# Attention stage of a two-layer encoder: the rotation in six operations over all ten heads, and the low halves of later input units subtracted on POOL

## The chip, the cores and the metric

The kernel runs on one core of one Trainium2 chip. A core has four compute engines, each with an instruction queue of its own that is worked off in order: PE (TensorE, the matrix unit), DVE (VectorE), ACT (ScalarE) and POOL (GpSimd). DMA transfers are issued from a queue too, here from SP (SyncE) and from POOL. The metric is device time of one execution in microseconds, the median over runs of the kernel.

## The reference, cut to what matters

The network has two layers. Layer 0 projects a modulated input `h = x * (1 + scale) + shift` once and feeds windowed attention, a spatial gate and a gating path from it; layer 1 is a bidirectional recurrence. The change touches layer 0: how `h` is split into two parts, and the rotation of queries and keys.

```python
S, D_MODEL, HEAD_DIM, N_Q_HEADS, N_KV_HEADS = 2048, 1024, 64, 8, 2
ROPE_DIM = HEAD_DIM // 4            # 16: only the first 16 of a head's 64 columns turn

def partial_rotary(t, positions):
    half = ROPE_DIM // 2
    ang = positions.astype(jnp.float32)[:, :, None, None] * inv_freq
    cos, sin = jnp.cos(ang), jnp.sin(ang)
    t1, t2 = tr[..., :half], tr[..., half:]
    rot = jnp.concatenate([t1 * cos - t2 * sin, t2 * cos + t1 * sin], axis=-1)
    return jnp.concatenate([rot.astype(t.dtype), t[..., ROPE_DIM:]], axis=-1)

def even_mixer(h, positions, w_in, w_out, sink, ...):
    q, k, v, su, sv, g = jnp.split(h @ w_in, EVEN_SPLITS, axis=-1)
    q = partial_rotary(q.reshape(B, S, N_Q_HEADS, HEAD_DIM), positions)
    k = partial_rotary(k.reshape(B, S, N_KV_HEADS, HEAD_DIM), positions)
    y_attn = windowed_gqa_sink(q, k, v, sink)      # |i - j| <= 128, softmax with a sink per head
    y_sg = chunked_spatial_gating(su, sv, ...)
    y = jnp.concatenate([y_attn, y_sg], axis=-1) * jax.nn.silu(g)
    return y @ w_out
```

## The kernel before, in words

All products of 32-bit numbers are made from two parts: a number is split into a high part `hi` (rounded to the matrix unit's fp32r type) and a low part `lo`, the number less `hi`. The helper `split` (L147) writes `hi` on ACT and `lo` on DVE, and `mm3` (L151) adds three matmuls, hi by hi (L152), hi by lo (L153) and lo by hi (L154).

Attention works on 16 blocks of 128 tokens. Its parts are:

- `build(u)` makes the input unit `u`, which is 256 tokens or two blocks: in four pieces of 256 features it loads x (L319), transposes it on PE (L325), applies scale and shift on ACT into the tile `hm` (two buffers), splits it into `hhi` and `hlo`, and stores both to memory for a later stage (L336, queue SP). There are eight units.
- `project(blk)` multiplies a block's `hi` and `lo` by the weights: keys and values first (`pk`, 256 columns), then the eight query heads (`pq`, 512 columns). ACT copies the results into the tile `qk`, heads 0 to 7 queries and 8 to 9 keys. DVE rotates 16 columns of each head (L365 to L370), in six operations for the two key heads and then six for the eight query heads. The keys are split into `ks` (L374 on ACT, L375 on DVE), transposed on PE (L379) and copied to `kT` (L387).
- `scores(blk)` splits and transposes the queries (L411 to L415), multiplies them by the keys (L422, L423), and makes the softmax: DVE takes mask and minimum (L424), ACT the exponential (L427), DVE the division (L434). DVE then transposes in squares of 32 (L452), and 16 DMAs move the squares from T to P (L459), for blocks 0 to 10 half of them issued by SP and half by POOL, for later blocks all by SP. Blocks 14 and 15 are transposed on PE instead (L444).
- `values(blk)` multiplies by the values (L469), copies out on ACT (L477), and POOL issues the store (L479).

The order in the text, from L494 on, is: units 0 and 1 are built during the setup together with the modulation and the split of the weights; then for each block in turn `scores(blk + 1)`, for even blocks `build((blk + 4) // 2)`, `values(blk)`, `project(blk + 3)`. This is not the order of each engine's queue: `schedule_with_timeline_sim=True` (L1194) lets a planner, which follows a model of the times, place the instructions of every queue before the program is made. What a queue holds is then fixed.

Once attention's projections are over, the loads of `h` for the next stage start (L521, L522), behind what stands in SP's queue. The later stages are the spatial gate with the output projection, and the recurrence of layer 1.

Of the kernel before, what the change touches and what calls it, by code (L numbers as in the profile page):

```python
# [7 lines left out]
F32 = mybir.dt.float32  # L8
F32R = mybir.dt.float32r
I32 = mybir.dt.int32  # L10
AF = mybir.ActivationFunctionType
ALU = mybir.AluOpType
# [41 lines left out]
def kernel(  # L54
# [27 lines left out]
    nc = tc.nc  # L82
    act = nc.scalar.activation
    tt = nc.vector.tensor_tensor
# [9 lines left out]
    def pool(stack, name, side=None, bufs=1, space=None):  # L94
        kw = {} if space is None else {"space": space}
        if side is not None:
            kw["side"] = side
        return stack.enter_context(tc.tile_pool(name=name, bufs=bufs, reuse_waits="tile", **kw))
# [48 lines left out]
    def split(hi, lo, src):  # L147
        act(out=hi, in_=src, func=AF.Copy)  # L148
        tt(out=lo, in0=src, in1=hi.bitcast(F32), op=ALU.subtract)  # L149

    def mm3(ps, ahi, alo, bhi, blo, first, last):  # L151
        nc.tensor.matmul(ps, lhsT=ahi, rhs=bhi, start=first, stop=False)  # L152
        nc.tensor.matmul(ps, lhsT=ahi, rhs=blo, start=False, stop=False)  # L153
        nc.tensor.matmul(ps, lhsT=alo, rhs=bhi, start=False, stop=last)  # L154

    def bank(p, tag, shape=(128, C)):
        t = p.tile(list(shape), F32, tag=tag, name=tag)
        return t
# [74 lines left out]
    for i in range(2):  # L233
        nc.gpsimd.dma_start(out=vrow0[24 + 8 * i:32 + 8 * i].rearrange("k (a q) -> k a q", a=4),
                            in_=ada_b[1, i * D:i * D + D].rearrange("(a k q) -> k a q", a=4, q=32))
# [22 lines left out]
    cos_t = ap.tile([128, 16, 8], F32, name="cos_t")  # L258
    sin_t = ap.tile([128, 16, 8], F32, name="sin_t")
# [43 lines left out]
    def k_place(n, p):  # L303
        if n not in kTs:
            kTs[n] = ap.tile([128, 4, 768], F32R, tag="kT", bufs=2, name="kT")
        return kTs[n][:, :, p * 128:p * 128 + 128]
# [7 lines left out]
    def build(u, part=range(4)):  # L314
        t, uu = divmod(u, 2)
        hT = hTs.setdefault(u, ([], []))
        for k2 in part:
            xp = jp.tile([128, 2, 256], F32, tag="xp", bufs=2, name="xp")
            load(out=xp, in_=xs[u * 256:u * 256 + 256, k2 * 256:k2 * 256 + 256].rearrange("(b p) f -> p b f", p=128))  # L319
            hi = jp.tile([128, 2, 256], F32R, tag="act", bufs=18, name="hhi")  # L320
            lo = jp.tile([128, 2, 256], F32R, tag="act", bufs=18, name="hlo")
            ps = bank(px, "px", (128, 2, 256))
            for j in range(2):
                for b in range(2):
                    nc.tensor.transpose(ps[:, j, b * 128:b * 128 + 128], xp[:, b, j * 128:j * 128 + 128], ident)  # L325
            h = jp.tile([128, 2, 256], F32, tag="hm", bufs=2, name="hm")
            for j in range(2):
                k = 2 * k2 + j
                act(out=h[:, j], in_=ps[:, j], func=AF.Identity, scale=scale[:, 0, k:k + 1],
                    bias=shift[:, 0, k:k + 1])  # L330
            split(hi, lo, h)
            for j in range(2):
                hT[0].append(hi[:, j])
                hT[1].append(lo[:, j])
            for d, r in zip(h_d[t], (hi, lo)):
                store(out=d[:, 2 * k2:2 * k2 + 2, uu * 256:uu * 256 + 256], in_=r.bitcast(F32))  # L336

    def project(blk):
        if blk >= NB:
            return  # L340
        hT = hTs[blk // 2]
        sl = slice(blk % 2 * 128, blk % 2 * 128 + 128)
        pk = bank(pj, "pj")
        for k in range(KD):
            mm3(pk[:, 0:256], hT[0][k][:, sl], hT[1][k][:, sl], wqh[:, k, 512:768], wql[:, k, 512:768], k == 0,
                k == KD - 1)
        pq = bank(pj, "pj")
        for k in range(KD):
            mm3(pq, hT[0][k][:, sl], hT[1][k][:, sl], wqh[:, k, 0:512], wql[:, k, 0:512], k == 0, k == KD - 1)
        qk = ap.tile([128, 10, 64], F32, tag="qk", bufs=4, name="qk")  # L350
        qkb[blk] = qk
        act(out=qk[:, 8:10, :], in_=pk[:, 0:128].rearrange("p (h d) -> p h d", h=2), func=AF.Copy)
        vt = ap.tile([128, 128], F32, tag="vt", bufs=7, name="vt")
        vts[blk] = vt
        act(out=vt, in_=pk[:, 128:256], func=AF.Copy)
        act(out=qk[:, 0:8, :], in_=pq.rearrange("p (h d) -> p h d", h=8), func=AF.Copy)
        rot = ap.tile([128, 4, 10, 8], F32, tag="rot", bufs=2, name="rot")
        for h0, h1 in ((8, 10), (0, 8)):
            n = h1 - h0
            cb = cos_t[:, blk:blk + 1, :].to_broadcast([128, n, 8])  # L360
            sb_ = sin_t[:, blk:blk + 1, :].to_broadcast([128, n, 8])
            t1 = qk[:, h0:h1, 0:8]
            t2 = qk[:, h0:h1, 8:16]
            r0, r1, r2, r3 = (rot[:, i, h0:h1, :] for i in range(4))
            tt(out=r0, in0=t1, in1=cb, op=ALU.mult)  # L365
            tt(out=r1, in0=t2, in1=sb_, op=ALU.mult)
            tt(out=r2, in0=t2, in1=cb, op=ALU.mult)
            tt(out=r3, in0=t1, in1=sb_, op=ALU.mult)
            tt(out=t1, in0=r0, in1=r1, op=ALU.subtract)
            tt(out=t2, in0=r2, in1=r3, op=ALU.add)  # L370
        ks = ap.tile([128, 4, 128], F32R, tag="ks", bufs=2, name="ks")
        kf = qk[:, 8:10, :]
        kd = ks[:, 0:2, :].rearrange("p k (u d) -> p k u d", u=2)
        act(out=kd, in_=kf[:, :, None, :].to_broadcast([128, 2, 2, 64]), func=AF.Copy)  # L374
        tt(out=ks[:, 2:4, :].rearrange("p k (u d) -> p k u d", u=2),  # L375
           in0=kf[:, :, None, :].to_broadcast([128, 2, 2, 64]), in1=kd.bitcast(F32), op=ALU.subtract)
        ps = bank(px, "px")
        for i in range(4):
            nc.tensor.transpose(ps[:, i * 128:i * 128 + 128].bitcast(F32R), ks[:, i, :], ident_r)  # L379
        n, p = divmod(blk, 4)  # L380
        places = [(n, p + 1)]
        if p == 0 and n > 0:
            places.insert(0, (n - 1, 5))
        if p == 3 and blk < NB - 1:
            places.append((n + 1, 0))
        for place in places:
            act(out=k_place(*place), in_=ps.rearrange("p (i n) -> p i n", i=4), func=AF.Copy)  # L387
# [101 lines left out]
    for n in range(2):  # L489
        modulation(Ring(ap, st, "P", 3, 4), (psc, "psc"), "aw", 0, 0, n, wide=wide)  # L490
        modulation(Ring(ap, st, "P", 3, 4), (psc, "psc"), "aw", 0, 1, n, wide=wide)
        build(0, range(2 * n, 2 * n + 2))
        split_w(range(4 * n, 4 * n + 4))
        build(1, range(2 * n, 2 * n + 2))  # L494
    ss.close()
    tq = pool(sb, "shuf", right)
    tail = []
    project(0)
    project(1)
    scores(0)  # L500
    project(2)
    for blk in range(NB):
        scores(blk + 1)
        if blk % 2 == 0 and blk + 4 < NB:
            build((blk + 4) // 2)
        values(blk)
        project(blk + 3)
        if blk + 3 == NB - 1:
            spj.close()
            cp = pool(sa, "work", left)  # L510
            tail.append(pool(sb, "tail", left))
# [134 lines left out]
    for i in range(4):  # L646
        stt(out=bias_sg[:, i, :], in0=ps[:, i * 128:i * 128 + 128], scalar=vcol0[:, 52 + i:53 + i],
            in1=bias_sg[:, i, :], op0=ALU.mult, op1=ALU.add)
# [473 lines left out]
    op = pool(ctx, "outp", right)  # L1122
# [76 lines left out]
```

## Time and profile before

| what | value |
|---|---|
| median of three runs | 1581.41 us (1581.18 to 1595.87) |
| profiled execution, its own time | 1584.51 us |
| its span (first to last instruction) | 1582.8 us |
| busy in the span: PE, DVE, ACT, POOL | 94%, 77%, 49%, 26% |
| mean granted PE clock | 0.98 |

The profile of one execution is read as follows. A row of a timeline is: start in us from the span's start, duration, engine and line, operation, output tile, input tiles, shape, number of instructions taken together, and in brackets how long the engine was idle before it and what ended that. PE is the matmul and PEld the weight load that overlaps it. SPq is SP's queue as it issues a DMA. A row of a table of stretches gives the length, then for each engine its busy time and (x) its instructions. The ends of matmuls are modelled, so that a busy PE isn't always a PE at its peak. Instructions on one engine are pipelined: a row may start before the one in front of it has ended. Attention's steady part runs from about 55 to 282 us.

### The profile page before, as it was taken

To read this page: it belongs to the slowest core of one execution; us is meant where nothing else is said; L and a number is where in the kernel's file an instruction comes from. 1 tells how busy PE (TensorE), PEld (TensorE's weight loads), DVE (VectorE), ACT (ScalarE), POOL (GpSimd) and SP (SyncE) were. 2 spreads that over 40 slices of the span, in tenths; PEclk is the share of its full clock that TensorE was granted. 3 is DMA by queue.
4 is the path that set the end of the run, shared out by engine and by line. 5 is a ranking of instruction groups with operands and counts; after the bars stand their busy time and mean duration, and the time that the engine had idled before them with its cause. 6 is when DMAs were issued, how large, how long until landed. Compare 5 with 4: busy or idle time off the path is not lost.

```text
span 1582.8 us, 21904 instructions
## 1 busy us (share of the span) xinstructions
PE 1491.3 (94%) x7096; PEld 1186.1 (75%) x7096; DVE 1218.3 (77%) x2212; ACT 782.8 (49%) x1458; POOL 416.8 (26%) x480
## 2 busy tenths in 40 slices
PE   6999999899999999999999899998998999889997
PEld 3887777557877777788877788777776778777886
DVE  4499888755769568966867767988998987887794
ACT  4677767442423333343344238388686686861100
POOL 1023231002005000300120233647656644112121
PEclk9999999899999999999999999999999999989999
DMA  9357876749798989978775698776676567549662
GB/s 346 125 170 220 227 193 181 235 139 300 243 287 293 245 262 307 321 261 285 275 250 166 198 273 246 225 229 225 211 220 211 199 201 250 186 180 336 240 221 86
DMA packets 204601, 366.72 MB, mean 232 GB/s; under 512 B 54568, under 2 KB 100804, under 8 KB 204488
## 3 DMA queue, kind: packets, MB, share of 16 engines
q1 hardware_dynamic: 198888, 352.71, 69.2%
q0 software_dynamic: 5600, 12.62, 3.1%
q8 instruction: 56, 0.92, 0.2%
q14 instruction: 57, 0.47, 0.1%
HBM read 264.07 MB, written 79.68 MB: 217 GB/s over the span
## 4 chain that ended last, share of the span: by engine, by line
PE 48%; DVE 19%; DMA 15%; ACT 8%; issue 5%; SPq 3%; POOL 1%; DVEq 0%; POOLq 0%; ACTq 0%
PE pj L152 8%; PE pj L153 8%; PE pj L154 8%; DMA raw<-in_ev_w_in_dram 3%; DMA praw<-in_od_w_in_dram 3%; PE po L469 3%; DVE hl L149 2%; PE pm L152 2%; DVE xc L941 2%; PE pm L153 2%; PE pm L154 2%; DMA raw<-in_ev_w_out_dram 2%; DMA praw<-in_od_w_out_dram 2%; ACT ra L976 1%; PE px L154 1%
## 5 line engine op out<-in xcount | busy, mean ns | idle before, releaser
L148 ACT ACTIVATE hl<-raw 128x512 fp32r<-128x512 f32 x192 | 118.6, 628 | 218.4 <-DMA raw<-in_ev_w_in_dram 140.1
L152 PE MATMUL pj<-ahi,hl 128*128 128x512 f32 x512 | 199.9, 393 | 4.9 <-ACT G L912 3.9
L153 PE MATMUL pj<-alo,hl 128*128 128x512 f32 x512 | 201.1, 393 | 0.0
L154 PE MATMUL pj<-ahi,hl 128*128 128x512 f32 x512 | 200.3, 393 | 0.0
L149 DVE TENSOR_TENSOR hl<-raw,hl 128x512 fp32r<-128x512 f32 x192 | 131.8, 697 | 66.7 <-ACT hl L148 66.4
L144 POOL TENSOR_SCALAR rstd<-mv 128x1 f32<-128x1 f32 x32 | 30.9, 964 | 473.3 <-DVE mv L610 362.6
L152 PEld LDWEIGHTS pj<-ahi,hl 128*128 128x128 f32 x512 | 97.0, 189 | 26.5 <-ACT G L912 4.3
L154 PEld LDWEIGHTS pj<-ahi,hl 128*128 128x128 f32 x512 | 97.0, 189 | 20.8
L153 PEld LDWEIGHTS pj<-alo,hl 128*128 128x128 f32 x512 | 96.9, 189 | 20.4
L424 DVE CUSTOM_DVE_ANT_0 P<-psc,mask,nsink 128x384 f32<-128x384 f32 (+1 forms) x128 | 73.8, 596 | 23.5 <-PE psc L423 23.4
L152 PE MATMUL pj<-wqh,hhi 128*128 128x256 f32 (+1 forms) x256 | 89.2, 353 | 2.6 <-ACT hhi L148 1.9
L153 PE MATMUL pj<-wql,hhi 128*128 128x256 f32 (+1 forms) x256 | 88.6, 347 | 0.0
L148 ACT ACTIVATE phl<-praw 128x512 fp32r<-128x512 f32 x56 | 35.4, 632 | 105.4 <-DMA praw<-in_od_w_in_dram 51.2
L154 PE MATMUL pj<-wqh,hlo 128*128 128x512 f32 (+1 forms) x256 | 86.1, 348 | 1.5 <-DVE hlo L149 1.4
L459 POOL DMA_DIRECT2D P<-T x88 | 49.0, 565 | 143.6 <-DVE nm L424 79.0
L427 ACT ACTIVATE P<-P,nm 128x384 f32<-128x384 f32 (+1 forms) x128 | 76.5, 601 | 16.0 <-DVE nm L424 15.9
L148 ACT ACTIVATE ahi<-yt 128x512 fp32r<-128x512 f32 (+1 forms) x44 | 32.2, 743 | 100.1 <-DVE yt L1095 61.3
L1005 POOL TENSOR_TENSOR T<-T 128x512 f32<-128x512 f32 (+2 forms) x32 | 60.4, 1889 | 79.2 <-DVE T L996 42.9
L771 POOL TENSOR_TENSOR alo<-hm,ahi 128x512 fp32r<-128x512 f32 x32 | 49.3, 1547 | 118.0 <-DVE hm L770 96.6
L941 DVE SCALAR_TENSOR_TENSOR xc<-X,vcol,xc 128x512 f32<-128x512 f32 (+2 forms) x96 | 74.0, 794 | 0.2
L971 DVE SCALAR_TENSOR_TENSOR ii<-ii,xc 128x1024 f32<-128x1024 f32 (+2 forms) x32 | 42.7, 1334 | 37.9 <-ACT ii L965 37.9
L152 PE MATMUL pm<-xhi,hg 128*128 128x512 f32 (+3 forms) x160 | 56.8, 370 | 14.3 <-ACT ra L960 7.5
(296 smaller groups left out, 4355.0 us busy)
## 6 DMA issues: line engine op xcount, KB each, us to landing
hl<-w_d SPq DMA_DIRECT2D x128, 512.0 KB, 4.6
raw<-in_ev_w_in_dram SPq DMA_DIRECT2D x128, 256.0 KB, 4.0
w_d<-phl SPq DMA_DIRECT2D x40, 512.0 KB, 4.5
aw<-in_ada_w_dram SPq DMA_DIRECT2D x32, 512.0 KB, 6.0
hg<-w_d SPq DMA_DIRECT2D x32, 512.0 KB, 4.3
P<-T SPq DMA_DIRECT2D x128, 96.0 KB, 3.7
aw<-in_ada_w_dram SPq DMA_DIRECT2D x8, 1024.0 KB, 8.0
xp<-in_x_dram SPq DMA_DIRECT2D x32, 256.0 KB, 3.0
```

Source lines behind the costliest of these rows:

```text
L148: act(out=hi, in_=src, func=AF.Copy)
L149: tt(out=lo, in0=src, in1=hi.bitcast(F32), op=ALU.subtract)
L152: nc.tensor.matmul(ps, lhsT=ahi, rhs=bhi, start=first, stop=False)
L153: nc.tensor.matmul(ps, lhsT=ahi, rhs=blo, start=False, stop=False)
L154: nc.tensor.matmul(ps, lhsT=alo, rhs=bhi, start=False, stop=last)
L424: nc.vector.tensor_tensor_reduce(out=p[:, g, 0:W], in0=ps[:, 0:W], in1=mask[:, m0:m0 + W], scale=-0.125, scalar=nsink[:, h:h + 1], op0=ALU ...
L427: act(out=p[:, g, 0:W], in_=p[:, g, 0:W], func=AF.Exp, scale=-1.0, bias=nm[:, h:h + 1], accum_out=rs[:, h:h + 1])
L459: dma.dma_start(out=pv[32 * r:32 * r + 32, 0:nb, i], in_=T[32 * i:32 * i + 32, 0:nk].rearrange("p (j r) m -> p r j m", r=4)[:, r])
L469: nc.tensor.matmul(ops[64 * kv:64 * kv + 64, :], lhsT=vts[lo_b + j][:, 64 * kv:64 * kv + 64], rhs=pv[:, j, kv] if blk >= PE_FROM else pv[: ...
L771: nc.gpsimd.tensor_tensor(out=lo[:, j], in0=h, in1=hi[:, j].bitcast(F32), op=ALU.subtract)
L941: stt(out=xc[:, w], in0=xt[:, j0 + j:j0 + j + W], scalar=vcol1[:, 8 * j + g:8 * j + g + 1], in1=xc[:, w], op0=ALU.mult, op1=ALU.add)
L1005: nc.gpsimd.tensor_tensor(out=T[i][:, 0, w], in0=T[i][:, 0, w], in1=T[i][:, 1, w], op=ALU.add)
```

## The change

There are two edits. In `build`, units 0 and 1 make `lo` on DVE as before; units 2 to 7 make it on POOL, with the same operation and the same operands. In `project`, the rotation is done once over all ten heads, in six operations in place of twelve; it reads both `pk`'s and `pq`'s copies.

```diff
@@ build
-            split(hi, lo, h)
+            act(out=hi, in_=h, func=AF.Copy)
+            (nc.vector if u < 2 else nc.gpsimd).tensor_tensor(out=lo, in0=h, in1=hi.bitcast(F32), op=ALU.subtract)
@@ project
-        for h0, h1 in ((8, 10), (0, 8)):
-            n = h1 - h0
-            cb = cos_t[:, blk:blk + 1, :].to_broadcast([128, n, 8])
-            sb_ = sin_t[:, blk:blk + 1, :].to_broadcast([128, n, 8])
-            t1 = qk[:, h0:h1, 0:8]
-            t2 = qk[:, h0:h1, 8:16]
-            r0, r1, r2, r3 = (rot[:, i, h0:h1, :] for i in range(4))
-            (six tt on these)
+        cb = cos_t[:, blk:blk + 1, :].to_broadcast([128, 10, 8])
+        sb_ = sin_t[:, blk:blk + 1, :].to_broadcast([128, 10, 8])
+        t1 = qk[:, :, 0:8]
+        t2 = qk[:, :, 8:16]
+        r0, r1, r2, r3 = (rot[:, i] for i in range(4))
+        tt(out=r0, in0=t1, in1=cb, op=ALU.mult)
+        tt(out=r1, in0=t2, in1=sb_, op=ALU.mult)
+        tt(out=r2, in0=t2, in1=cb, op=ALU.mult)
+        tt(out=r3, in0=t1, in1=sb_, op=ALU.mult)
+        tt(out=t1, in0=r0, in1=r1, op=ALU.subtract)
+        tt(out=t2, in0=r2, in1=r3, op=ALU.add)
```

More of the change, by code (lines that the diff above doesn't have):

```diff
@@ L357, in project @@
         rot = ap.tile([128, 4, 10, 8], F32, tag="rot", bufs=2, name="rot")
-        for h0, h1 in ((8, 10), (0, 8)):
-            n = h1 - h0
-            cb = cos_t[:, blk:blk + 1, :].to_broadcast([128, n, 8])
-            sb_ = sin_t[:, blk:blk + 1, :].to_broadcast([128, n, 8])
-            t1 = qk[:, h0:h1, 0:8]
-            t2 = qk[:, h0:h1, 8:16]
-            r0, r1, r2, r3 = (rot[:, i, h0:h1, :] for i in range(4))
[L365 to L370, printed above, removed]
+        cb = cos_t[:, blk:blk + 1, :].to_broadcast([128, 10, 8])
[9 more added lines that the diff above has]
+        tt(out=t2, in0=r2, in1=r3, op=ALU.add)
         ks = ap.tile([128, 4, 128], F32R, tag="ks", bufs=2, name="ks")
```

## Prediction

> **What bounds the kernel now.** I read the page first, for the engines and the chain, and then, of the attention stage alone, the table by stretches.
>
> ```profile
> span 1582.8 us, 21904 instructions
> PE 1491.3 (94%) x7096; PEld 1186.1 (75%) x7096; DVE 1218.3 (77%) x2212; ACT 782.8 (49%) x1458; POOL 416.8 (26%) x480
> PE 48%; DVE 19%; DMA 15%; ACT 8%; issue 5%; SPq 3%; POOL 1%; DVEq 0%; POOLq 0%; ACTq 0%
> ```
>
> PE is the engine of the kernel, and half of the chain that ended last is its work. All that the change edits runs in the steady part of attention, where two blocks and one input unit make one period. Four of them, cut where the values' matmuls (L469) of every second block start:
>
> ```profile
> core 0: us, PE busy (x) PEld busy (x) DVE busy (x) ACT busy (x) POOL busy (x), PEclk, DMA share, GB/s
> 133.30:165.80 32.50, 32.30 (x191) 24.89 (x192) 29.08 (x94) 24.12 (x67) 10.41 (x18) 1.00 0.76 206
> 165.80:198.80 33.00, 32.98 (x195) 25.28 (x195) 29.41 (x100) 23.91 (x67) 10.37 (x18) 1.00 0.76 212
> 198.80:232.40 33.60, 33.32 (x199) 26.22 (x199) 30.41 (x100) 24.88 (x70) 10.31 (x18) 1.00 0.74 205
> 232.40:266.10 33.70, 32.02 (x192) 25.11 (x193) 29.69 (x100) 25.39 (x71) 10.23 (x18) 1.00 0.68 188
> sum 132.80, PE 130.63 PEld 101.50 DVE 118.58 ACT 98.29 POOL 41.33; mean PE 32.66 PEld 25.38 DVE 29.64 ACT 24.57 POOL 10.33
> ```
>
> The reader is to see two things. PE is idle for only 132.80 - 130.63 = 2.17 us in four periods, 1.68 of them in the last. And DVE is almost as full: it has 3.19 to 4.01 us to spare in a period. So the change takes work from the second fullest engine, not from the one that bounds. What PE lost to DVE is in the waits (here from 55 to 290 us):
>
> ```profile
> PEld pj L154 <- DVE hlo L149: 3.0, 5, 1.7
> PEld psc L422 <- DVE nm L424: 2.8, 10, 0.8
> PE pj L154 <- DVE hlo L149: 1.4, 1, 1.4
> ```
>
> These are the largest: 3.0 + 2.8 = 5.8 us on the weight load, most of it hidden behind a running matmul, and 1.4 us on PE itself, 7.2 together. The one long wait:
>
> ```profile
> 249.84 1.78 DVE L452 STREAM_TRANSPOSE T<-P 128x1536 f32<-128x1536 f32 x1
> 251.58 0.69 DVE L149 TENSOR_TENSOR hlo<-hm,hhi 128x512 fp32r<-128x512 f32 x1
> 252.32 0.39 PE L154 MATMUL pj<-wqh,hlo 128*128 128x256 f32 x1 [1.40 <-DVE hlo L149]
> ```
>
> Here the low half stood behind a transpose of the softmax in DVE's queue, and PE stood still until it came. Such waits are what the change can win.
>
> **Edit 1, the rotation.** Durations on DVE overlap, so I price by starts.
>
> ```profile
> 129.45 0.17 DVE L365 TENSOR_TENSOR rot<-qk,cos_t 128x16 f32<-128x16 f32 x1
> 129.54 0.17 DVE L366 TENSOR_TENSOR rot<-qk,sin_t 128x16 f32<-128x16 f32 x1
> 144.51 0.22 DVE L365 TENSOR_TENSOR rot<-qk,cos_t 128x64 f32<-128x64 f32 x1
> 144.65 0.22 DVE L366 TENSOR_TENSOR rot<-qk,sin_t 128x64 f32<-128x64 f32 x1
> ```
>
> An operation over 16 columns takes 0.09 us, one over 64 takes 0.14, so a column costs about 0.05 / 48 = 0.001. A block pays 6 x 0.09 + 6 x 0.14 = 1.38 us before, and 6 x (0.14 + 0.016) = 0.94 after. That is 0.44 us less DVE time a block, 0.9 in a period, 7 us over 16 blocks.
>
> What moves is the key's rotation: it now waits for the queries' projection too. Who is late then? I followed the second block of a period:
>
> ```profile
> 139.92 0.43 DVE L375 TENSOR_TENSOR ks<-qk,ks 128x256 fp32r<-128x256 f32 x1 [0.49 <-ACT ks L374]
> 143.26 0.60 ACT L356 ACTIVATE qk<-pj 128x512 f32<-128x512 f32 x1 [2.13 <-PE pj L154]
> 147.07 3.43 DVE L452 STREAM_TRANSPOSE T<-P 128x1536 f32<-128x1536 f32 x2
> 155.12 0.45 PE L379 MATMUL px<-ident_r,ks 128*128 128x128 f32 x4
> ```
>
> Its queries are copied at 143.26 to 143.86, its joint rotation could end by about 147, where the query's did, and the key's split, with the long transpose in front of it, by about 151. PE transposes the keys only at 155.12, so some 4 us are left, and the edit costs nothing there. Without that cover the key's chain would end where PE's last query matmul ends plus 0.6 (copy), 0.94, 0.4 and 0.4 (split), about 2.4 us of exposed time a block if PE had nothing else queued. In the first block of a unit the keys' and queries' matmuls are interleaved and end together, so there is nothing to wait for.
>
> **Edit 2, the low halves.** Six units of four pieces are 24 operations.
>
> ```profile
> 151.47 0.69 DVE L149 TENSOR_TENSOR hlo<-hm,hhi 128x512 fp32r<-128x512 f32 x1
> 152.07 0.61 DVE L424 CUSTOM_DVE_ANT_0 P<-psc,mask,nsink 128x384 f32<-128x384 f32 x1
> 152.21 0.19 PEld L154 LDWEIGHTS pj<-wqh,hlo 128*128 128x128 f32 x1 [0.31 <-DVE hlo L149]
> L771 POOL TENSOR_TENSOR alo<-hm,ahi x32: 1284/1481/2212, 867.3 to 1269.6; 128x512 fp32r<-128x512 f32 x32
> ```
>
> By starts one takes DVE 0.60 us: 2.4 us less in a period, 14.4 in all. The same operation of the same shape stands on POOL in a later stage: shortest 1.28, median 1.48, longest 2.21 us. I take the median: 5.9 us more POOL time a period, 35.5 in all (31 to 53). POOL has 32.5 - 10.41 = 22 us to spare in a period, so throughput is no question. Latency is: a low half takes 0.8 us longer, and the third row shows that PE picks one up as soon as it ends (152.16, then 152.21). POOL's queue matters as well:
>
> ```profile
> 148.44 0.64 ACT L148 ACTIVATE hhi<-hm 128x512 fp32r<-128x512 f32 x1
> 149.43 0.65 ACT L148 ACTIVATE hhi<-hm 128x512 fp32r<-128x512 f32 x1
> 149.86 0.71 POOL L479 DMA_DIRECT2D o_d<-oq  x1 [9.10 <-ACT oq L477]
> 151.11 4.34 POOL L459 DMA_DIRECT2D P<-T  x8 [0.53 <-DMA h_d<-hhi]
> 151.46 7.11 SPq L459 DMA_DIRECT2D P<-T  x8
> ```
>
> When `hhi` of the first two pieces are ready (149.1 and 150.1), POOL has been idle for most of 9.10 us. Those two would end near 151 and 153; DVE ended the first at 152.16. The third may come behind the eight issues, which end at 155.45, and end one length later, near 157: up to 1.5 us late. The issues themselves may slip by 1.5 to 3 us, but SP issues the other eight until 158.57, 3.1 us after POOL, so this is covered. SP's store of a low half (L336) waits for POOL now; behind it in SP's queue are loads of x and the next P<-T, with the same 1 to 2 us at stake. ACT writes `hm` again only when the low half is made: two buffers, and the first two come no later.
>
> **The price of POOL beside DVE.** The trace shows it in the later stage:
>
> ```profile
> 867.30 3.17 POOL L771 TENSOR_TENSOR alo<-hm,ahi 128x512 fp32r<-128x512 f32 x2 [64.69 <-DVE hm L770]
> 865.42 1.29 DVE L149 TENSOR_TENSOR alo<-yt,ahi 128x512 fp32r<-128x512 f32 x2
> 867.54 3.48 DVE L149 TENSOR_TENSOR hl<-raw,hl 128x512 fp32r<-128x512 f32 x2
> ```
>
> Two subtractions that take DVE 1.29 us took 3.48 while POOL ran two of its own: 2.2 us lost for 3.17 of POOL, and DVE came free about when POOL did. So a low half on POOL can hold DVE for at most its own length. The Trainium skill states this as a lock ("SBUF — State Buffer", section "Who interferes with whom"): a DVE instruction with two inputs in SBUF and a POOL instruction that reads SBUF exclude each other, and so does DVE in a two-port mode; the trace agrees by the 3.48. By that rule the masking (L424, one input from PSUM) goes on beside POOL, and the rotation and the splits don't.
>
> The bounds for DVE in a period: nothing lost at best; at worst 4 x 1.48 = 5.9 us against 2.4 + 0.9 = 3.3 won, 2.6 more than before, which still fits into 3.19 to 4.01 of idle time. Much of DVE's work there is masking and transposes, and I take half of the worst, 3.0: DVE comes out 0.3 us better a period, which is next to nothing.
>
> **The sum.** PE's own work is unchanged. On the path at most the 2.17 us in four periods, or 3.05 from 55 to 282 us:
>
> ```profile
> 55.00:282.00 227.00, 223.95 (x1334) 178.78 (x1334) 193.86 (x677) 165.88 (x468) 57.18 (x99) 1.00 0.64 179
> 282.00:347.00 65.00, 55.47 (x236) 34.30 (x233) 37.28 (x101) 28.07 (x75) 2.85 (x4) 0.92 0.59 178
> 275.93 0.24 PE pj L154
> 267.93 10.83 SPq L459 DMA_DIRECT2D P<-T  x16
> 280.46 0.38 SPq L521 DMA_DIRECT2D ahi<-h_d  x1
> ```
>
> I take 2 us of it. A second term is at the end of attention: SP's 16 transfers start at 267.93 behind a DVE transpose, and the loads for the next stage behind them at 280.46; PE's last projection, whose space they take, ends at 276.2, so a DVE that is ahead could pull these loads forward by up to 4 us. I take 1. The new latency on PE (the third piece, some 1.5 us, six times, at most 9) is not taken off, because the planner places other matmuls in front. So -3 us on the profiled 1584.5, that is 1581.5. That execution lies 3.1 us above the median of 1581.4; the forecast for the median is 1578. My forecast's own range against no change is -8 (the 7.2 of waits, or 4 + 4 of both terms) to +9 (the third pieces): 1573 to 1590.
>
> **The rivals.**
>
> *POOL's queue holds the low halves (slower).* If the planner puts a piece behind the eight issues, and its matmuls early in PE's queue, PE waits 4.34 us plus 0.8 for each unit: 6 x 5.1 = 31 us, 1609. It decides as soon as a piece ends more than PE's queue in front of it lasts; for it speaks the 152.21 above (no slack) and the 1.40 wait, in which PE had nothing else; against it the 9.10 us of idle POOL in front, and that the issues come after the transposes, when two pieces are done. If it strikes every second unit, 1594.
>
> *The lock takes back what DVE won.* DVE is then 2.6 us worse a period; if all of it reached PE, 6 x 2.6 = 16 us: 1594 or, as far as the 3 us and more of idle time cover it, the forecast's gain lost, 1581. The Trainium skill's rule, named above, would lead here.
>
> *DVE was the true pace.* Then all those waits (7.2) and the idle time of the end of attention (65.00 - 55.47 = 9.5) go: 1581 - 17 = 1564. Against it: the end waits for transfers, which are not fewer.
>
> *The edit does nothing on the path*: 1581. And since the planner makes all queues anew, later stages may be ordered differently; I know no row for that, and allow 5 us either way.
>
> **How the numbers follow.** The forecast gets 0.55, no effect or the lock within its cover 0.21, the queue or an uncovered lock 0.15 (half of it over 1597), DVE as the pace 0.09. One per cent is 16 us, about what a measurement of this kernel can tell from no change. Faster by more, under 1566: 0.08. Slower by more, over 1597: 0.11. Within: 0.81. The range leaves out the outermost parts of the last two cases: 1567 to 1594.
>
> **What would show it.** In the changed profile the twelve rotation rows of a block are six of 128x80 at about 0.24 us; 24 subtractions stand on POOL at 1.3 to 2.2; DVE's busy time in a period falls from 29.6 to between 27 and 29; and the periods stay at 32 to 33.5 us. The forecast is wrong if PE shows waits for POOL's `hlo` of over 1 us for each unit, if the periods grow past 35, or if the stages after 347 us take other than 1236 us.

## The result, and the profile after

The kernel became slower: 1645.95 us (median, 1641.13 to 1647.98) against 1582.41 for before on the same chip, a ratio of 1.0365 [1.0336, 1.0394]. By the medians that is 64 us more, and far outside the range forecast. Ratios, here and below, are taken over fast runs against those of before on the same chip, with 95% intervals, and can differ a little from the quotient of two medians (here 1.040).

The head of the page of the kernel after (span, then busy time of each engine):

```profile
span 1645.8 us, 21812 instructions
PE 1514.9 (92%) x7096; PEld 1197.2 (73%) x7096; DVE 1215.6 (74%) x2092; ACT 786.9 (48%) x1458; POOL 451.5 (27%) x504
```

The reader is to see that no engine has more matmuls or operations to work through, but for POOL. PE has the same 7096 matmuls, though it is busy for 1514.9 us with them, 23.6 more than before; DVE is 2.7 us less busy. The rest of the time is idle time. The table by stretches, before and then after, shows where:

```profile
55.00:345.00 290.00, 277.42 (x1562) 212.21 (x1561) 231.14 (x777) 193.36 (x541) 60.03 (x103) 0.98 0.63 180
150.00:200.00 50.00, 49.98 (x301) 39.45 (x301) 45.35 (x146) 36.75 (x105) 15.29 (x27) 1.00 0.81 227
```

```profile
55.00:345.00 290.00, 244.38 (x1319) 185.04 (x1319) 192.40 (x554) 168.36 (x463) 87.67 (x124) 0.94 0.51 144
100.00:150.00 50.00, 41.80 (x214) 29.80 (x215) 32.08 (x84) 25.73 (x70) 21.53 (x32) 0.90 0.65 182
150.00:200.00 50.00, 41.30 (x222) 30.73 (x223) 32.67 (x100) 29.01 (x80) 15.12 (x22) 0.93 0.53 152
200.00:250.00 50.00, 40.76 (x219) 29.76 (x216) 34.66 (x98) 28.88 (x81) 15.85 (x23) 0.93 0.51 143
```

In 50 us PE now does some 218 matmuls where it did 301, and it stands for 8 to 9 us of them. By the 195 matmuls of a period before, a period has grown from 33 to 195 / 218 x 50 = 45 us. In the trace the last of attention's matmuls with the values ends at 408.4 us, where before it was 346.2; what comes behind takes 1237.4 us, before 1236.6. So the loss lies in the attention stage, which ends 62.2 us later. From 55 us to that end PE stood for 52.0 us, before for 12.6, and was busy for 301.4 us, before for 278.6, with as many matmuls to within a few. So some 39 of the 62 us are idle time, and some 23 are matmuls that took longer: the granted clock over this time is 0.92, before 0.98 (the last section shows how). What PE waits for (waits of the kernel after, 55 to 400 us: sum, times, longest):

```profile
PE px L325 <- DMA xp<-in_x_dram: 31.8, 8, 7.3
PE psc L421 <- DVE nm L423: 5.3, 6, 3.6
```

The longest sum is a wait that before hardly had: for the input x. And there is no row of PE waiting for POOL's low half, the wait that I had feared. Before, the loads of x and the transposing issues around them stand so in SP's queue:

```profile
102.41 7.86 SPq L459 DMA_DIRECT2D P<-T  x8
112.13 0.89 SPq L319 DMA_DIRECT2D xp<-in_x_dram  x2
117.45 0.88 SPq L319 DMA_DIRECT2D xp<-in_x_dram  x2
118.94 8.15 SPq L459 DMA_DIRECT2D P<-T  x8
```

Two of the eight waits of the kernel after, in the timelines of SP's queue and PE:

```profile
108.97 20.99 SPq L458 DMA_DIRECT2D P<-T  x16
130.05 1.06 SPq L319 DMA_DIRECT2D xp<-in_x_dram  x2
168.69 7.36 SPq L458 DMA_DIRECT2D P<-T  x8
177.32 1.01 SPq L319 DMA_DIRECT2D xp<-in_x_dram  x2
134.64 1.94 PE L325 MATMUL px<-ident,xp 128*128 128x128 f32 x8 [4.82 <-DMA xp<-in_x_dram]
171.18 0.63 PE L325 MATMUL px<-ident,xp 128*128 128x128 f32 x4 [1.28 <-ACT P L426]
180.62 1.08 PE L325 MATMUL px<-ident,xp 128*128 128x128 f32 x4 [7.04 <-DMA xp<-in_x_dram]
```

Before, SP loads x between two groups of eight transposing issues. Now it takes 20.99 us over sixteen of them, some 5 us of it standing between the two groups, and only then loads the next x, which PE is waiting for. So its queue is in another order than before, and so are the others: matched by operation, tiles and shape in the two traces, 1199 of PE's 1764 matmuls up to the end of attention stand in common order, while all 5332 behind it do. The question for the experiments was then whether the operations or the order cost the 64 us.

### The profile page after: what moved, and what is told of

Read it like the earlier page. It is cut to its first block, busy times and chain, and to the rows that moved or that the text cites. A ratio compares the mean times of both kernels' runs of the same rounds, so it can differ in the third digit from the quotient of the medians.

```text
span 1645.8 us, 21812 instructions
## 1 busy us (share of the span) xinstructions
PE 1514.9 (92%) x7096; PEld 1197.2 (73%) x7096; DVE 1215.6 (74%) x2092; ACT 786.9 (48%) x1458; POOL 451.5 (27%) x504
## 4 chain that ended last, share of the span: by engine, by line
PE 47%; DVE 19%; DMA 15%; ACT 8%; issue 5%; SPq 3%; POOL 1%; DVEq 0%; ACTq 0%; POOLq 0%
PE pj L152 7%; PE pj L153 7%; PE pj L154 7%; PE po L468 3%; DMA praw<-in_od_w_in_dram 2%; DMA raw<-in_ev_w_in_dram 2%; PE pm L152 2%; DMA aw<-in_ada_w_dram 2%; PE pm L153 2%; DVE xc L940 2%; PE pm L154 2%; DVE hl L149 2%; PE px L153 2%; PE px L154 2%; PE px L152 2%
## 5 line engine op out<-in xcount | busy, mean ns | idle before, releaser
L154 PEld LDWEIGHTS pj<-ahi,hl 128*128 128x128 f32 x512 | 97.4, 190 | 20.8
L152 PE MATMUL pj<-wqh,hhi 128*128 128x512 f32 (+1 forms) x256 | 90.9, 358 | 5.1 <-ACT hhi L331 4.3
L153 PE MATMUL pj<-wql,hhi 128*128 128x512 f32 (+1 forms) x256 | 90.0, 352 | 0.0
L1004 POOL TENSOR_TENSOR T<-T 128x512 f32<-128x512 f32 (+2 forms) x32 | 64.3, 2009 | 79.2 <-DVE T L995 42.9
L153 PE MATMUL pm<-xlo,hg 128*128 128x512 f32 (+3 forms) x160 | 57.3, 359 | 11.0 <-DVE xlo L149 11.0
```

The costliest lines, as they stand in the source:

```text
L1004: nc.gpsimd.tensor_tensor(out=T[i][:, 0, w], in0=T[i][:, 0, w], in1=T[i][:, 1, w], op=ALU.add)
```

## The experiments

### Each edit alone, and the order of the rotation alone, planned anew

The first kernel has the six joint rotations only, the second the subtractions on POOL only; both edits are those of the diff above. The third keeps twelve operations and turns their order:

```diff
-        for h0, h1 in ((8, 10), (0, 8)):
+        for h0, h1 in ((0, 8), (8, 10)):
```

> Before with the joint rotation alone (six operations over ten heads); the low halves stay on DVE. Theory A (the joint rotation ties the key's split to the query's projection, the planner then lays out the period anew, and PE's transposes of x come to stand in PE's queue ahead of loads that SP issues late): most of the +64 us is here, 1620 to 1650, PE waits for x of 20 us and more in attention. Rival B (the low halves on POOL do it, by their latency, the lock, or their place in POOL's and SP's queues): 1575 to 1590 here.

> Before with the low halves of units 2 to 7 on POOL alone; the rotation stays in twelve operations. Theory A: near before, 1575 to 1595. Rival B: 1620 to 1650, with PE waiting for x or for the low halves. If both this and the rotation alone are slow, either edit upsets the planner's order.

> Before with the twelve rotation operations in the other order, the queries' six first and then the keys' six: the same operations, the same work, but the key's split now waits for the query's projection as it does with the joint rotation. Theory A: slower, towards the time of the joint rotation alone (over 1600). Rival (the planner's order depends on the number of operations and not on the wait): within 1 per cent of before, 1570 to 1597.

Measured: joint rotation 1599.3 us, 1.0055 [1.0013, 1.0098]; subtractions on POOL 1615.84, 1.0188 [1.0156, 1.0219]; turned order 1588.5, 1.0014 [0.9995, 1.0033]. The first two lie between the ranges of their theory and their rival, the third in its rival's. Both edits cost, the rotation by little more than the measurement can tell, and 0.55% + 1.88% is less than the 3.65% of the two together. That keys come after queries costs nothing that can be measured when the planner may place the rest to suit.

### Operations and order, crossed

To part the two I held the order. A function `hold`, called once where the text of the attention stage ends, puts an edge without a wait between neighbours of a queue, from a list of instructions in the order that another kernel's queue had:

```diff
     sb.close()
+    hold(tc)
...
+def hold(tc):
...
+    for queue in table.values():
...
+        for a, b in zip(queue, queue[1:]):
+            tc.add_manual_dep(traced[b], a, mybir.DependencyInfo(
+                mybir.DependencyClass.NoSync, mybir.DependencyReason.DATA), reason="held order")
```

The first kernel has the subtractions on POOL and every other instruction in before's order. The second does the work of before in the order of the kernel with the subtractions on POOL.

> The low halves of units 2 to 7 on POOL, the rotation as before, and every other instruction of PE, ACT, DVE, SP and POOL held in exactly the order of the kernel before (edges on the same queue, no waits). POOL's low halves stand where the prediction put them: the first in front of a store, the second behind it, the third and fourth behind the eight issues. Theory A2 (what costs is the new order that the planner makes, not POOL's time): 1572 to 1590, as the prediction's sum for this edit. Rival B (POOL's latency, its queue or its lock with DVE): 1605 to 1625, the time of the edit with its own order (1616).

> The reverse: exactly the work of the kernel before (low halves on DVE), with PE, ACT, SP, POOL's DMAs and DVE's other instructions held in the order that the planner made for the low halves on POOL. Theory A2: slow, 1605 to 1630. Rival B: near before, 1580 to 1592.

Measured: POOL in the old order 1599.99 us, 1.0072 [1.0049, 1.0095]; the old work in the new order 1618.34, 1.0184 [1.0143, 1.0225]. The second equals the 1.0188 of the edit itself: an order made for the edit makes its loss without the edit. But the edit isn't free in the old order either: 1599.99 lies between the two ranges expected. Its waits on PE, and one of them in the timelines of PE, POOL and DVE:

```profile
PE pj L154 <- POOL hlo L332: 11.2, 6, 3.1
```

```profile
157.17 1.33 POOL L332 TENSOR_TENSOR hlo<-hm,hhi 128x512 fp32r<-128x512 f32 x1
158.41 4.35 POOL L460 DMA_DIRECT2D P<-T  x8
162.78 1.28 POOL L332 TENSOR_TENSOR hlo<-hm,hhi 128x512 fp32r<-128x512 f32 x1
164.36 1.40 POOL L332 TENSOR_TENSOR hlo<-hm,hhi 128x512 fp32r<-128x512 f32 x1 [0.30 <-ACT hhi L331]
164.11 0.39 PE L154 MATMUL pj<-wqh,hlo 128*128 128x256 f32 x1 [0.98 <-POOL hlo L332]
158.07 0.46 DVE L430 TENSOR_TENSOR es<-nm,nsink 128x4 f32<-128x4 f32 x1
161.44 3.17 DVE L435 TENSOR_SCALAR P<-P,rs 128x384 f32<-128x384 f32 x4
166.02 1.41 DVE L435 TENSOR_SCALAR P<-P,rs 128x384 f32<-128x384 f32 x4
```

Six waits, one for each unit on POOL, 11.2 us in all, about as much as the 0.72% (11 us). The mechanism is the one of my first rival: a piece stands behind the eight issues, the third in five units and the second in the first unit, and PE takes it as it ends (164.06, then 164.11). The waits are not all of it. In this profiled execution attention ends at 364.8 us, 18.6 later than before: PE stood for 12.7 us more, the transposed P (8.9 us, before 4.2) among the causes, and its matmuls took 5.8 us longer, at a granted clock of 0.96.

The last three rows show the lock. The small operation at 158.07 ends only when POOL's of 157.17 has ended. Four scalings that take DVE 1.41 us take 3.17 when POOL works beside them: the third of them runs from 162.87 to 164.28, past the end of POOL's subtraction of 162.78, and takes 1.41 us alone. (The first takes 1.13 us beside POOL's last issues, before that subtraction starts; so not all of the 3.17 is the subtraction's.) Over the stage, the operations of DVE that overlapped one of these subtractions took 19.3 us more than the median of the same operation elsewhere: 10.5 us of it in eight scalings, the rest in operations with two inputs in memory. Twelve maskings (0.57 to 0.61 us) and seven transposes (1.73 to 1.77) took what they take elsewhere. The scaling has one tensor in memory as its input; the Trainium skill ("SBUF — State Buffer", section "Who interferes with whom") counts it among the operations that can take the shared ports in their two-port modes, and the 1.41 us of the third scaling agree.

### Both edits near the old order, the rotation alone in it, and two pieces only

The first two hold all queues in before's order from block 1 on and leave the key's split, transposes and copy (L374 to L387) to the planner. The third is the held kernel of the last section with the third and fourth piece of a unit back on DVE:

```diff
-            (nc.vector if u < 2 else nc.gpsimd).tensor_tensor(out=lo, ...)
+            (nc.gpsimd if u > 1 and k2 < 2 else nc.vector).tensor_tensor(out=lo, ...)
```

> Both edits, with the queues of PE, ACT, DVE, SP and POOL's DMAs held in the order of the kernel before from block 1 on to the last block's projection; the rotation stands where the queries' six operations stood, and the key's split (L374, L375 of before) is free; the ends of the stage are the planner's. Theory A2 (the new order is the larger part of the +64 us): 1590 to 1610, that is the +12 us of the low halves on POOL in that order and a few for the rotation. Rival (the two edits cost by their own operations and waits, order or not): 1630 to 1650.

> The joint rotation alone, held in the same way. Prediction's step (7 us less on DVE, the key's chain covered): 1575 to 1588. Rival (the key's chain is exposed): 1595 to 1610, more than the joint rotation with its own order (1599).

> Low halves on POOL for the first two of the four pieces of units 2 to 7 alone (the third and fourth stay on DVE), every other instruction of the attention stage in the order of the kernel before, rotation as before. If the +12 us of the held kernel with all four on POOL are the third piece that stands behind the eight issues in POOL's queue, they vanish: 1578 to 1590. If they are POOL's lock with DVE or its longer operation, half or more stays: 1592 to 1600.

Measured: both edits 1605.37 us, 1.0119 [1.0093, 1.0145]; rotation alone 1596.36, 1.0072 [1.0051, 1.0094]; two pieces on POOL 1594.1, 1.0052 [1.0031, 1.0073]. The first lies in the theory's range, the second in the rival's, and the third in the range for the lock or the longer operation. So some 20 of the 64 us (20.1 by the medians) are what both edits cost near the old order, and the other 43 or so came with the planner's new one. What PE waits for, with both edits, and then the longest wait of the rotation alone:

```profile
PE pj L154 <- POOL hlo L332: 7.0, 5, 2.5
PE px L378 <- ACT ks L373: 6.9, 2, 6.0
```

```profile
92.63 0.23 DVE L368 TENSOR_TENSOR qk<-rot 128x80 f32<-128x80 f32 x1
92.90 0.42 ACT L372 ACTIVATE ks<-qk 128x256 fp32r<-128x256 f32 x1 [1.62 <-DVE qk L368]
93.37 0.49 PE L377 MATMUL px<-ident_r,ks 128*128 128x128 f32 x2 [3.49 <-ACT ks L372]
```

The rest of the own waits is the key's chain: with the rotation alone PE stood for 3.49 us until the joint rotation and the split were through. With both edits the two rows make 13.9 us, about the 13.3 by which PE stood longer than before up to the end of attention (25.8 us against 12.6); longer matmuls, at a clock of 0.97, make another 7.

With two pieces on POOL the wait for `hlo` fell to 2.3 us, once. But the time did not fall with it: 1594.1 us, and the interval overlaps the one of four pieces. Its profiled execution was the fastest of eight (1588.69 to 1600.42); there attention ended at 347.7 us, 1.5 after before, and the span is 4.2 us above before's, 2.7 of them after attention, where its later stages had come out in another order. So the piece behind the issues is shown as a wait, but not how much of the 0.72% it makes, and the 0.52% is not wholly accounted for. It is no better than before, nor is any other kernel of this study.

### The order of both edits, with the old work

Before's subtractions and its twelve rotations, and every queue in the order that the kernel after has (TensorE's, ScalarE's and SyncE's exactly):

> The work of before (subtractions on VectorE, rotation in twelve operations), with every engine's queue held in the order that the kernel with both edits has; VectorE's own extra rotation operations stand beside the ones they belong to. Theory (the planner's new order of the attention stage is what costs, some 45 us of the 64): 1625 to 1650 us, with the attention stage ending between 390 and 410 us. Rival (the operations cost, the order little): 1585 to 1600 us. Between them, 1600 to 1625, the two would act together.

Measured: 1646.11 us, 1.038 [1.0347, 1.0413]. Its row of the table by stretches and its longest wait on PE:

```profile
55.00:345.00 290.00, 245.78 (x1320) 186.09 (x1319) 197.78 (x665) 167.97 (x462) 56.78 (x100) 0.92 0.51 144
```

```profile
PE px L325 <- DMA xp<-in_x_dram: 33.3, 8, 7.2
```

Compare 244.38 and 31.8 of the kernel after. Attention ends at 406.5 us. The whole loss, 60.5 us by the medians, is there without either edit. It also says that the two costs don't add: in the new order the operations themselves cost nothing more.

### Is it the wait for x?

The longest wait suggested a remedy: a third buffer for x in the kernel after, so that loads can be issued earlier.

```diff
-            xp = jp.tile([128, 2, 256], F32, tag="xp", bufs=2, name="xp")
+            xp = jp.tile([128, 2, 256], F32, tag="xp", bufs=3, name="xp")
```

> The changed kernel with three buffers for x in place of two, planned anew. If PE's waits for x (34 us in the changed kernel) come from loads that SP can't issue until a buffer is free, they fall by half or more and the time to 1600 to 1625; if they come from the place of the loads in SP's queue behind other transfers, they stay and so does the time, 1635 to 1655.

Measured: 1645.05 us, 1.0363 [1.0308, 1.0418]: nothing. PE's wait for x, 31.8 us in the kernel after, now reads

```profile
PE px L325 <- DMA xp<-in_x_dram: 15.6, 5, 8.3
```

So the wait fell by half, as the first theory has it, and the time stayed, as the second has it. From 55 us to the end of attention PE stood for 48.4 us, where it was 52.0: other waits took its place, the one for the transposed P (8.5 us, where it was 1.9) first.

### Which queue?

The kernel after, with one or two queues held in before's order and the others planned anew around them. First SyncE alone and TensorE alone:

> Both edits, with the queue of SyncE alone (the loads of x, the stores and half of the transposing DMAs) held in the order of before; every other queue is ordered anew by the planner around it. If the loads of x behind fifteen transposing DMAs are the cause, the time falls to 1605 to 1620 us; if SyncE's order is only one expression of a poorer order of TensorE's queue, it stays between 1630 and 1650 us.

> Both edits, with the queue of TensorE alone held in the order of before; the others are ordered anew by the planner around it. Theory (the order in which TensorE takes projections, transposes of x and scores is what costs): 1595 to 1615 us, near the kernel with both edits and all queues held (1605). Rival (VectorE's or the DMA queues' order costs): 1625 to 1650 us.

Measured: SyncE held 1642.31 us, 1.0348 [1.0314, 1.0382], so SP's order alone isn't the cause; TensorE held 1636.32, 1.0311 [1.0281, 1.0341]. My theory for the second (1595 to 1615) fell. The waits on PE, SyncE held and then TensorE held:

```profile
PE po L468 <- DMA P<-T: 16.4, 6, 5.3
PE px L325 <- DMA xp<-in_x_dram: 10.3, 7, 2.3
```

```profile
PE px L325 <- DMA xp<-in_x_dram: 27.7, 5, 7.8
PE px L378 <- ACT ks L373: 10.8, 3, 6.1
```

With the loads in the old places PE waits for the transposed P instead; with PE in the old order, the loads of x are late again. So I held two (the joint rotation has no place in the old order; where VectorE's queue is held, it and the key's split are left to the planner):

> Both edits, with the queues of TensorE and of SyncE held in the order of before; VectorE, ScalarE and POOL are ordered anew by the planner around them. Theory (the two queues have to fit each other: TensorE's order says when a piece of x is needed, SyncE's when it is loaded): 1600 to 1618 us, where each of the two held alone gave 1636 and 1642. Rival (the loss sits in VectorE's order of masking, transposes and splits): 1625 to 1645 us.

> Both edits, with the queues of TensorE and of VectorE held in the order of before, but for the key's split, which the planner places; ScalarE, SyncE and POOL are ordered anew around them. Theory (TensorE and SyncE have to fit): SyncE is free again, so 1620 to 1640 us. Rival (TensorE and VectorE have to fit): 1600 to 1618 us. Should both this kernel and the one with TensorE and SyncE held fall to 1600 to 1618 us, then a second queue in the old order, whichever it is, draws the rest after it.

Measured: TensorE and SyncE 1629.45 us, 1.0276 [1.0249, 1.0303], so this theory fell too; TensorE and VectorE 1611.06, 1.0178 [1.0152, 1.0204], the range of the rival. Waits on PE of the first, and then of the second:

```profile
PE px L378 <- ACT ks L373: 16.4, 4, 6.1
PE psc L443 <- DVE nm L423: 5.3, 1, 5.3
PE psc L421 <- DVE nm L423: 5.3, 5, 2.3
```

```profile
PE px L378 <- ACT ks L373: 10.2, 5, 3.2
PE pj L154 <- POOL hlo L332: 7.4, 5, 2.9
PE pja L153 <- DVE hl L149: 5.3, 1, 5.3
```

The wait for x is gone from both, but in the first PE waits for the key's split and for maskings that VectorE, now in an order of its own, does late. The second has the waits that both edits have near the old order, and one of 5.3 us for a split at the next stage's first projection. Is it VectorE's order alone?

> Both edits, with the queue of VectorE alone held in the order of before, but for the key's split; TensorE, ScalarE, SyncE and POOL are ordered anew around it. If VectorE's order is what costs, TensorE's following from it: 1605 to 1620 us, near the 1611 of TensorE and VectorE held together. If the two have to fit each other: 1625 to 1645 us, as with TensorE held alone (1636).

Measured: 1643.42 us, 1.0356 [1.0317, 1.0395]. No: its longest wait on PE is

```profile
PE psc L421 <- DVE nm L423: 18.0, 9, 5.3
```

TensorE's new order asks for the scores' space when VectorE's old order hasn't freed it. So of the queues tried, the two have to fit each other, and SyncE follows. With both held, its queue loads x in two pairs a unit, ahead of the next eight transposing issues, although nothing holds it:

```profile
125.01 0.89 SPq L319 DMA_DIRECT2D xp<-in_x_dram  x2
...
130.35 0.94 SPq L319 DMA_DIRECT2D xp<-in_x_dram  x2
...
131.89 8.39 SPq L458 DMA_DIRECT2D P<-T  x8
```

Together they bring back about half of the loss (3.65% to 1.78%); all queues near the old order bring it to 1.19%.

What stays open: why the planner, for such small edits, chose an order in which even the old work takes some 60 us longer, was not tried, since no trace shows its model. Pairs without TensorE were not tried either.

## Why the prediction was wrong

**The step that failed** is the last item of the rivals: "since the planner makes all queues anew, later stages may be ordered differently; I know no row for that, and allow 5 us either way". I priced a new order as noise, and looked for it in the later stages. There it was nothing: 1236.6 and 1237.4 us, with all of PE's 5332 matmuls in the order of before, so that the stated test of 1236 was met. In the attention stage, where the edit is, the new order with the old work alone made some 60 us (1646.11 against 1585.60), and both edits near the old order made some 20. All else was worked out as though the rows of before would stay in their places. My own condition, periods past 35 us, came true with 45.

**The third piece** was sized a little low ("some 1.5 us, six times, at most 9") and then "not taken off, because the planner places other matmuls in front". In the old order nothing was in front for long enough: six waits of 1.0 to 3.1 us, 11.2 in all. The rival's placement (a piece behind the eight issues) was right and its price of 31 us was too high, as two of four pieces come first in most units: piece, store, piece, issues, piece, piece. In the kernel after, the wait is absent: its pieces stand elsewhere among the issues, and in one unit POOL itself stood for 2.71 and 4.38 us before the third and the fourth piece (177.98 and 183.62) until ACT had made `hhi`. That this is why is not shown.

**The key's chain** had "some 4 us" of cover. I had followed one block, the second of a period in the steady part. With the rotation alone in the old order PE waited for the key's split for up to 3.49 us, and that kernel lost 0.72%. The price without cover, 2.4 us, was of the right order; the cover was taken from one block for all.

**What was right.** The six joint operations and POOL's subtractions, in the timeline and the groups of the kernel after:

```profile
151.97 0.23 DVE L365 TENSOR_TENSOR rot<-qk,sin_t 128x80 f32<-128x80 f32 x1
152.12 0.24 DVE L366 TENSOR_TENSOR rot<-qk,cos_t 128x80 f32<-128x80 f32 x1
152.28 0.23 DVE L367 TENSOR_TENSOR rot<-qk,sin_t 128x80 f32<-128x80 f32 x1
```

```profile
L332 POOL TENSOR_TENSOR hlo<-hm,hhi 128x512 fp32r<-128x512 f32 x24 | 31.1, 1306 | 117.1 <-ACT hhi L331 102.4 <-issue 11.3 <-DMA P<-T 3.3
```

By starts a rotation takes 0.16 us as worked out; a subtraction takes 1.31, less than the 1.48 that I took. The lock was real and of about the size assumed. The page of the kernel with the subtractions on POOL in the old order:

```profile
PE 1495.1 (93%) x7096; PEld 1189.3 (74%) x7096; DVE 1224.7 (77%) x2188; ACT 782.3 (49%) x1458; POOL 450.3 (28%) x504
```

DVE lost 14.4 us of work and is busy for 6.4 us more than the 1218.3 of before: 20.8 us came back, 19.3 of them in the operations that overlapped POOL's subtractions, where half of the worst, 3.0 a period, makes 18 over six. So edit 2 took nothing off DVE at all. That the masking goes on beside POOL was right too. The claim that DVE's busy time in a period falls to 27 to 29 us isn't met: 33.1 us in 50 make 29.6 in a period of 195 matmuls, what it was.

**The waits to be won** (7.2 us at most) and the end of attention (up to 4 us) are not seen in any kernel: no version ended attention earlier than before. One slip in the rivals changes nothing: 1609 and 1594 are counted from the forecast's 1578, 1564 from the 1581 of before.

## What to carry to other kernels

Where a planner places the queues, an edit is two changes: the operations, and a new order of everything beside them. Here the order alone cost some 60 us, and the operations near the old order some 20. Measure them apart by holding the order (the edit in the old order, and the old work in the new order) before a duration is blamed, and don't take the engine that PE waits for as the cause: here the wait moved from x to P to the key's split as one queue after the other was put back. And work handed from an engine to a slower one with issues in its queue is late at the piece behind those issues, while DVE need not get the time back.

## What was not expected of the hardware

PE's granted clock fell in the kernel after, and the table by stretches shows how, here around the wait of 7.04 us that ended at 180.62:

```profile
174.00:177.50 3.50, 0.00 (x0) 0.00 (x0) 3.36 (x14) 3.47 (x12) 1.28 (x2) 1.00 0.77 217
178.00:184.50 6.50, 3.88 (x15) 3.53 (x16) 5.46 (x6) 1.65 (x3) 2.12 (x2) 0.50 0.75 234
185.00:200.00 15.00, 15.00 (x88) 10.78 (x89) 4.66 (x19) 7.33 (x20) 4.91 (x9) 1.00 0.64 187
```

The clock (the third number from the end) is whole for the first 4 us in which PE stands, half after that and for the first 4 us in which PE works again, and whole behind it. Four transposes of x took 1.08 us after this wait; after one of 1.28 us they took 0.63 (rows above). The Trainium skill ("TensorE: Matmul & The Clock Gate", Part 1) says that the clock drops to half after an idle window of about 3.4 us and comes back after as much of work; the rows agree. So a long wait costs more than its length. Up to the end of attention, 0.92 over 353.4 us is about 57 us at half clock, where before 0.98 over 291.2 was about 12; half of the difference, an estimate of 23 us, agrees with the 22.8 us by which PE was busy longer, over a third of the loss.

And DVE's scaling by one column, with a single tensor as input, is held by POOL just as an operation with two inputs is: 1.41 us for one that takes 0.41 elsewhere.
